# The sample's rows of a differential attention: both components' queries in one stationary operand, one softmax for 128 rows, summed while the weights are turned

## The chip, the cores and the metric

One NeuronCore of a Trainium2 chip runs one launch of a whole encoder layer. The metric is device time in microseconds, the median of several runs. Engines: PE (TensorE, matmuls; PEld is its weight load), DVE (VectorE), ACT (ScalarE), POOL (GpSimd), SP (SyncE, which issues most DMAs).

## The reference

One layer of a hybrid encoder serves two groups: a prompt of 512 rows and a sample of 64 rows, with shared weights. After a projection the rows go through a gated-delta recurrence and, side by side with it, a differential attention; then come an output projection, an attention to a memory, and a feed-forward block. The change is in the differential attention: 4 heads, each with two components of 64 dimensions.

```python
def one(args):
    qi, pi = args
    s = jnp.einsum('bqhcd,bkhcd->bhcqk', qi.astype(jnp.float32), kf) * scale
    visible = k_pos[None, :] < ((pi // CHUNK + 1) * CHUNK)[:, None]
    s = jnp.where(visible, s, -jnp.inf)
    p = jax.nn.softmax(s, axis=-1)
    a = p[:, :, 0] - lam * p[:, :, 1]
    return jnp.einsum('bhqk,bkhe->bqhe', a, vf)
```

Two softmaxes, one per component, are combined as the first minus lambda times the second, and the result weighs the values. The sample's 64 rows attend to 256 cached keys and their own 64, so 320 keys, all visible.

## The kernel before

Everything is held transposed, with features on the 128 partitions and the 576 rows (512 prompt, then 64 sample) along the free axis. Weights come by DMA in blocks, are split into a high and a low part (`wh` by ACT on L161, `wl` by DVE on L162), and `project` multiplies both with the split rows, in two passes over 256 and 320 rows. The PSUM tile of a projection is called `pr`; its matmuls fill PE whenever nothing else does, and they stand on L107, as every matmul does (helper `mm`). Transposes stand on L113 (helper `tr`, by a multiplication with `ident`). PSUM has eight banks: three `pr`, two `ba`, and one each of `g0`, `g1` and `gs`.

A list scheduler sorts the instructions of each engine by dependences and its own cost estimates. So an edit in one place moves instructions of the neighbours, and each engine then runs its list strictly in order.

For each head `h`, `diff_project(h)` projects queries, keys and values. The sample's queries are copied by ACT (L976) out of the projection into `qz`, component 1 into partitions 0 to 63 of plane 0, component 2 into partitions 64 to 127 of plane 1; the other halves were set to zero by POOL. `qz` has one buffer, so the copies for the next head wait until PE has read it. `diff_head(h)` then takes the sample (t = 4) first, and four prompt tiles of 128 queries (t = 0 to 3). For each tile and component the scores go into bank `g1` or `g0` (component index 1 first), DVE takes the row's maximum (L1052) and scales it (L1053), ACT takes the exponential with the row's sum (L1055) into `p1` or `p0`. DVE inverts the sums (L1057), multiplies component 2's by minus lambda (L1058), scales `p1` (L1059) and adds scaled `p0` to it (L1060). PE turns the combined weights into a `ba` bank in blocks of 128 keys, ACT copies them to `aT` (L1067), PE multiplies with the values into `gs`, and ACT takes the squares' sum (L1075) and copies the rows to `an` (L1076). `finish` normalizes the head's rows (L1079, the POOL power on L208, L1081) and turns them; it runs when the next head reaches t = 1.

For t = 4 the stationary operand is a plane of `qz` with 128 columns: the last 128 rows of the sequence axis, of which the last 64 are the sample's. In parallel with the heads runs the sample's recurrent scan (`sample`), which shares the bank `gs` and ends with the DVE product on L808, behind a POOL power. After head 3, the split rows are turned back (L1107, L1108) and the memory's keys and values follow.

Of the kernel before, what the change touches and what calls it, by code (L numbers as in the profile page):

```python
# [10 lines left out]
AF = mybir.ActivationFunctionType  # L11
# [26 lines left out]
def hybrid_layer_kernel(  # L38
# [53 lines left out]
    def small(tag, shape, bufs=None, dt=F32):  # L92
        tag = SHARED.get(tag, tag)
        bufs = 1 if tag in ("vn", "on", "S", "qz") or tag[:-1] in ("At", "Dt", "Y") else 2
        return sp.tile(shape, dt, tag=tag, name=nm(tag), bufs=bufs)
# [840 lines left out]
    ckT, cvv = cv2[:, 0].rearrange("p b (c n) -> p (b c) n", n=PAST), cv2[:, 1]  # L936

    qs = [cp.tile([P, 2, T], F32R, tag=f"qz{i}", name=nm("qs")) for i in range(2)]
    qz = small("qz", [P, 2, P])
    with tc.issue_after(behind_keys[0]), tc.issue_after(behind_keys[1]):  # L940
        G.memset(qz[64:, 0, :], 0.0)
        G.memset(qz[:64, 1, :], 0.0)
        G.memset(vs[64:], 0.0)
    stacked = {}

    def diff_project(h):
        hs = slice(h * P, (h + 1) * P)
        if h < 2:
            qn = [od[:, 2 * h + j, :SEQ].bitcast(F32R) for j in range(2)]
        else:  # L950
            qn = [small(tag, [P, SEQ], dt=F32R) for tag in ("Y0", "Y1")]
        tags = ("kd", "vb", "X", "KQ") if h % 2 else ("At0", "At1", "Dt0", "Dt1")
        ks = [small(tag, [P, SEQ], dt=F32R) for tag in tags]
        stacked[h] = ks[:2], ks[2:]
        for kind, base in (("q", 2056), ("k", 2568), ("v", 3080)):
            def evac(b, a0, n, more):
                ts_ = slice(a0, a0 + n)
                t0 = slice(a0, min(a0 + n, SEQ))
                n0 = t0.stop - a0

                def parts(dst, src):
                    A.copy(dst[0][:, t0], src[:, :n0])
                    V.tensor_tensor(dst[1][:, t0], src[:, :n0], dst[0][:, t0].bitcast(F32), ALU.subtract)

                if kind == "q":
                    d = b
                    if more is not None:
                        d = qn[1][:, ts_].bitcast(F32)
                    with tc.high_priority():
                        if more is not None:  # L970
                            add_to(d, b, more)
                        parts(qn, d)
                    if a0:
                        for c in range(2):
                            R = slice(64 * c, 64 * c + 64)
                            A.copy(qz[R, c, :], d[R, n - P :])  # L976
                            for j in range(2):
                                nc.sync.dma_start(
                                    qs[h % 2][64 * j : 64 * j + 64, c, :SEQ].bitcast(F32), qn[j][R].bitcast(F32)
                                )  # L980
                    return
                d = small("zr", [P, 320])[:, :n] if kind == "v" else kdT[:, h, ts_]
                with tc.high_priority():
                    if more is not None:
                        add_to(d, b, more)
                    else:
                        V.tensor_copy(d, b)
                if kind == "k":
                    parts(stacked[h][0], d)
                    if a0:  # L990
                        first_, second_ = ([x.bitcast(F32) for x in pair_] for pair_ in stacked[h])
                        for j in range(2):
                            for R in (slice(0, 64), slice(64, P)):
                                nc.sync.dma_start(second_[j][R], first_[j][64:])
                        for j in range(2):
                            nc.sync.dma_start(first_[j][64:], first_[j][:64])
                bt = bank()
                for t in range(2):
                    tr(bt[:, t * P : (t + 1) * P], d[:, t * P : (t + 1) * P])
                if a0:  # L1000
                    tr(bt[:DEC, 256:384], d[:, 256:])
                src, t2 = bt[:, :256].rearrange("p (t d) -> p t d", t=2), slice(a0 // P, a0 // P + 2)
                if kind == "v":
                    A.copy(vtm[:, t2, hs], src)
                    if a0:
                        A.copy(vs[:DEC, h, :], bt[:DEC, 256:384])
                else:
                    ko = small("ko", [P, 3, P])
                    A.copy(ko[:, :2], src)
                    nc.sync.dma_start(o_dk_p[0, 0, a0 : a0 + 256, h, :].rearrange("(t p) d -> p t d", p=P), ko[:, :2])  # L1010
                    if a0:
                        A.copy(ko[:DEC, 2], bt[:DEC, 256:384])
                        nc.sync.dma_start(o_dk_s[0, 0, :, h, :], ko[:DEC, 2])

            project(weights(w2, base + h * P), xs, evac)
        nc.sync.dma_start(o_dv_p[0, 0, :, h, :].rearrange("(t p) d -> p t d", p=P), vtm[:, :, hs])
        nc.sync.dma_start(o_dv_s[0, 0, :, h, :], vs[:DEC, h, :])

    def diff_cache():
        ckr = [small("p0", [P, 512]), small("p1", [P, 512])]  # L1020
        nc.sync.dma_start(cvv, cache_diff_v[0, 0].rearrange("(b p) h d -> p b (h d)", p=P))
        for bi in range(2):
# [3 lines left out]
                tr(b[:, h * P : (h + 1) * P], ckr[bi][:, h * P : (h + 1) * P])  # L1026
            A.copy(ckT[:, :, bi * P : (bi + 1) * P], v4(b, 4))

    def diff_head(h, between):


        hs = slice(h * P, (h + 1) * P)
        so, co = tiny([P, 5], "ta"), tiny([P, 5], "ta")
        on = small("an", [P, 5, P])
        for t in (4, 0, 1, 2, 3):
            if t == 1:
                between()
            q0 = QT[t][0]
            nk = q0 + P if t < 4 else PAST + DEC
            nb = (nk + P - 1) // P  # L1040
            pr = {}
            mx, l = tiny([P, 2], "ta"), tiny([P, 2], "ta")
            for c in (1, 0):
                b = bank(f"g{c}")
                if t < 4:
                    for j in range(2):
                        mm(b[:, :nk], qs[h % 2][:, c, q0 : q0 + P], stacked[h][c][j][:, :nk], start=j == 0, stop=j == 1)
                    V.memset(b[:64, nk - 64 : nk], -1e30)
                else:
                    mm(b[:, :PAST], qz[:, c, :], ckT[:, h, :])  # L1050
                    mm(b[:, PAST:nk], qz[:, c, :], kdT[:, h, SEQ:T])
                V.tensor_reduce(mx[:, c : c + 1], b[:, :nk], AX.X, ALU.max)  # L1052
                V.tensor_scalar(mx[:, c : c + 1], mx[:, c : c + 1], -0.125, None, ALU.mult)  # L1053
                p = small(f"p{c}", [P, 512])
                A.activation(p[:, :nk], b[:, :nk], AF.Exp, bias=mx[:, c : c + 1], scale=0.125, accum_out=l[:, c : c + 1])  # L1055
                pr[c] = p
            V.reciprocal(l, l)  # L1057
            V.tensor_tensor(l[:, 1:2], l[:, 1:2], nlam, ALU.mult)  # L1058
            V.tensor_scalar(pr[1][:, :nk], pr[1][:, :nk], l[:, 1:2], None, ALU.mult)  # L1059
            V.scalar_tensor_tensor(pr[0][:, :nk], pr[0][:, :nk], l[:, 0:1], pr[1][:, :nk], ALU.mult, ALU.add)  # L1060
            if nk < nb * P:
                G.memset(pr[0][:, nk : nb * P], 0.0)
            bt = bank()
            aT = small("aT", [P, 4, P])
            for kb in range(nb):
                tr(bt[:, kb * P : (kb + 1) * P], pr[0][:, kb * P : (kb + 1) * P])
            A.copy(aT[:, :nb, :], v4(bt, nb))  # L1067
            po = bank("gs")[:, :P]
            for kb in range(nb):
                if t < 4:  # L1070
                    vv = vtm[:, kb, hs]
                else:
                    vv = cvv[:, kb, hs] if kb < 2 else vs[:, h, :]
                mm(po, aT[:, kb, :], vv, start=kb == 0, stop=kb == nb - 1)
            A.activation(pr[1][:, :P], po, AF.Square, accum_out=so[:, t : t + 1])  # L1075
            A.copy(on[:, t, :], po)  # L1076

        def finish():
            V.tensor_scalar(so, so, 1.0 / P, EPS, ALU.mult, ALU.add)  # L1079
            rpow(co, so)  # L1080
            V.tensor_tensor(on, on, co.unsqueeze(2).to_broadcast([P, 5, P]), ALU.mult)  # L1081
            b, b2 = bank(), bank()
            for t in range(4):
                tr(b[:, t * P : (t + 1) * P], on[:, t, :])
            tr(b2[:, :P], on[:, 4, :])
            for src, ts_ in ((b, slice(0, SEQ)), (b2[:, DEC:P], slice(SEQ, T))):
                A.activation(od[:, h, ts_], src, AF.Identity, scale=dn)

        return finish
# [566 lines left out]
```

## Time and profile before

| | |
|---|---|
| median of 3 runs | 982.89 us (981.1 to 982.91) |
| profiled execution | 983.15 us, span 981.0 us, granted PE clock 0.998 |
| PE busy | 963.2 us (98 %) |
| PEld busy | 889.8 us (91 %) |
| DVE busy | 695.8 us (71 %) |
| ACT busy | 541.2 us (55 %) |
| POOL busy | 57.5 us (6 %) |
| PE on the chain that ended last | 59 % of the span, 38 % of it projection matmuls (`pr`) |
| the four heads of the differential attention | about 250 to 367 us |

Read the shares as averages over stages. In the timeline, a row has a start, a duration, the engine, the line, the operation and `output<-inputs`, with `xN` records; `[x <-engine line]` at its end is idle time ahead of the row and what ended it. A plain f32 matmul leaves two records, a transpose or an `f32r` matmul one.

### The profile page before, as it was taken

The numbers are of one execution on the slowest core, as the hardware profiler recorded it, in microseconds if no ns is written. First come the engines' busy times: TensorE is split into PE (matmuls) and PEld (weight loads), VectorE is DVE, ScalarE is ACT, GpSimd is POOL, SyncE is SP. The second block draws the span as 40 slices with busy tenths as digits, with TensorE's granted clock in tenths as the row PEclk, the third lists the DMA queues.
The fourth block names the chain that finished last, engine by engine and source line by source line (L and its number), as shares of the span: only waits on it lengthen the run. The fifth ranks groups of instructions, "written<-read, shape, count | busy, mean of one in ns | idle before, by whom it ended". The sixth has DMA issues, their size and how long they took to land.

```text
span 981.0 us, 17018 instructions
## 1 busy us (share of the span) xinstructions
PE 963.2 (98%) x6403; PEld 889.8 (91%) x6403; DVE 695.8 (71%) x1552; ACT 541.2 (55%) x1226; POOL 57.5 (6%) x122
## 2 busy tenths in 40 slices
PE   9999999999999999999999999999999999999996
PEld 7999999888888778999999998999999999999996
DVE  6655777867777687666657887567767779978674
ACT  7665785434557675435445567665544455544444
POOL 3441010101000000000000000000000000000000
PEclk9999999999999999999999999999999999999999
DMA  7442432121644756341121523222222222322202
GB/s 212 121 129 76 113 105 65 33 55 45 173 132 126 232 164 193 87 129 44 44 64 44 140 73 89 88 86 87 86 86 86 87 87 87 87 87 86 65 23 96
DMA packets 124915, 96.01 MB, mean 98 GB/s; under 512 B 6204, under 2 KB 112846, under 8 KB 124322
## 3 DMA queue, kind: packets, MB, share of 16 engines
q1 hardware_dynamic: 124466, 94.28, 33.2%
q8 instruction: 50, 0.82, 0.3%
q10 hardware_dynamic: 368, 0.66, 0.2%
q14 instruction: 31, 0.25, 0.1%
HBM read 79.93 MB, written 9.75 MB: 91 GB/s over the span
## 4 chain that ended last, share of the span: by engine, by line
PE 59%; issue 2%; DVE 2%; ACT 1%; DMA 1%; POOL 0%; POOLq 0%; ACTq 0%; DVEq 0%; SPq 0%
PE pr L107 38%; PE ba L107 10%; PE g L107 6%; PE gs L107 4%; PE ba L113 1%; DMA r<-in_w_ff_dram 1%; DMA raw<-in_w_ff_dram 0%; ACT c L1448 0%; ACT u L1539 0%; DVE w L1302 0%; ACT w2h L1402 0%; ACT c L1447 0%; DVE u L1495 0%; ACT keep L1438 0%; DVE w2l L1403 0%
## 5 line engine op out<-in xcount | busy, mean ns | idle before, releaser
L107 PE MATMUL pr<-u,wh 128*128 128x320 f32 (+2 forms) x1240 | 326.0, 341 | 1.3 <-DVE zr L195 0.9
L107 PEld LDWEIGHTS pr<-u,wh 128*128 128x128 f32 x1240 | 211.5, 188 | 16.3 <-DVE zr L195 1.1
L107 PE MATMUL pr<-u,wl 128*128 128x256 f32 (+1 forms) x816 | 225.9, 300 | 0.0
L107 PEld LDWEIGHTS pr<-u,wl 128*128 128x128 f32 x816 | 150.0, 189 | 2.2 <-DVE wl L388 0.2
L162 DVE TENSOR_TENSOR wl<-raw,wh 128x1024 fp32r<-128x1024 f32 x65 | 79.5, 1223 | 51.5 <-ACT wh L161 51.3
L161 ACT CAST wh<-raw 128x1024 fp32r<-128x1024 f32 x65 | 68.3, 1050 | 58.1 <-PE pr L107 41.4
L107 PE MATMUL pr<-u,w2h 128*128 128x320 f32 (+1 forms) x384 | 98.6, 340 | 0.0
L1402 ACT CAST w2h<-r 128x512 fp32r<-128x512 f32 x56 | 34.7, 619 | 89.5 <-PE pr L107 86.3
L107 PE MATMUL pr<-f,w2h 128*128 128x320 f32 (+1 forms) x288 | 74.6, 341 | 0.8 <-DVE u L1489 0.7
L107 PEld LDWEIGHTS pr<-u,w2h 128*128 128x128 f32 x384 | 65.0, 188 | 4.6 <-issue 0.4
L107 PE MATMUL pr<-u,w2l 128*128 128x256 f32 (+1 forms) x256 | 65.2, 295 | 0.0
L1487 DVE TENSOR_TENSOR u<-u,pr 128x256 f32<-128x256 f32 x96 | 42.2, 448 | 17.0 <-PE pr L107 16.4
L107 PE MATMUL ba<-u,wl 128*128 128x288 f32 x360 | 53.0, 296 | 1.0 <-ACT keep L1438 0.9
L107 PEld LDWEIGHTS pr<-f,w2h 128*128 128x128 f32 x288 | 48.7, 188 | 5.2 <-issue 2.0
L107 PEld LDWEIGHTS ba<-u,wl 128*128 128x128 f32 x360 | 49.2, 188 | 1.7 <-ACT keep L1438 1.6
L107 PE MATMUL pr<-f,w2l 128*128 128x256 f32 (+1 forms) x192 | 48.8, 295 | 0.0
L107 PEld LDWEIGHTS pr<-u,w2l 128*128 128x128 f32 x256 | 46.9, 188 | 1.5
L208 POOL TENSOR_TENSOR tiny<-tiny,nhalf 128x1 f32<-128x1 f32 (+4 forms) x10 | 9.3, 932 | 645.2 <-DVE tiny L1555 532.2
L1403 DVE TENSOR_TENSOR w2l<-r,w2h 128x512 fp32r<-128x512 f32 x56 | 38.5, 687 | 11.3 <-ACT w2h L1402 11.0
L107 PE MATMUL pr<-wh,u 128*128 128x512 f32 x128 | 43.3, 403 | 0.0
L1447 ACT ACTIVATE c<-c 128x288 f32<-128x288 f32 x48 | 20.6, 443 | 29.4 <-DVE c L1446 29.4
L107 PEld LDWEIGHTS pr<-f,w2l 128*128 128x128 f32 x192 | 35.2, 188 | 1.1
(536 smaller groups left out, 2032.0 us busy)
## 6 DMA issues: line engine op xcount, KB each, us to landing
raw<-in_w_ff_dram SPq DMA_DIRECT2D x36, 512.0 KB
raw<-in_w_in_dram SPq DMA_DIRECT2D x28, 512.0 KB
r<-in_w_ff_dram SPq DMA_DIRECT2D x56, 256.0 KB
raw<-in_w_mem_k_dram SPq DMA_DIRECT2D x8, 512.0 KB
raw<-in_w_mem_v_dram SPq DMA_DIRECT2D x8, 512.0 KB
raw<-in_w_out_dram SPq DMA_DIRECT2D x8, 512.0 KB
raw<-in_w_mem_q_dram SPq DMA_DIRECT2D x8, 512.0 KB
raw<-in_w_mem_o_dram SPq DMA_DIRECT2D x8, 512.0 KB
```

The source lines that it names most:

```text
L107: i = nc.tensor.matmul(out, lhsT, rhs, start=start, stop=stop, skip_group_check=skip_group_check)
L113: i = nc.tensor.transpose(out, in_, ident[:n, :n])
L161: A.copy(wh, raw)
L162: V.tensor_tensor(wl, raw, wh.bitcast(F32), ALU.subtract)
L208: G.tensor_tensor(out, in_, bc(nhalf[: in_.shape[0], 0:1], list(in_.shape)), ALU.pow)
L1402: A.copy(wh, src)
L1403: V.tensor_tensor(wl, src, wh.bitcast(F32), ALU.subtract)
L1447: A.activation(c, c, AF.Relu)
L1487: V.tensor_tensor(am, am, b, ALU.add)
```

## The change

For the sample's rows, `diff_head` calls a new function. `qz` is now one 128 x 128 operand in two diagonal blocks: component 1's 64 queries in rows and columns 0 to 63, component 2's in 64 to 127. Its product with the keys gives the scores of both components in one bank, component 1 in the upper 64 rows and component 2 in the lower. One maximum, one exponential, one reciprocal and one scaling then serve all 128 rows, the lower 64 with minus lambda. The two components are added by the turn: instead of a transpose (multiplication by the identity), a plain f32 matmul multiplies by `both`, whose columns 64 to 127 hold an identity for the upper rows and one for the lower, and whose other columns are zero. The result has the sample's rows in columns 64 to 127 of `aT`, as before, and zeros in the rest. What follows is unchanged, but for the name of the buffer that takes the squares. Prompt tiles are computed as before.

```diff
-    qz = small("qz", [P, 2, P])
+    qz = small("qz", [P, P])
+    both = const([P, P], "both")
     with tc.issue_after(behind_keys[0]), tc.issue_after(behind_keys[1]):
-        G.memset(qz[64:, 0, :], 0.0)
-        G.memset(qz[:64, 1, :], 0.0)
+        G.memset(qz[64:, :64], 0.0)
+        G.memset(qz[:64, 64:], 0.0)
+        G.memset(both[:, :64], 0.0)
+        for c in range(2):
+            G.tensor_copy(both[64 * c : 64 * c + 64, 64:], ident[64 * c : 64 * c + 64, 64 * c : 64 * c + 64])
...
-                            A.copy(qz[R, c, :], d[R, n - P :])
+                            A.copy(qz[R, R], d[R, n - DEC :])
...
+    def sample_rows(h, hs, so, on):
+
+        nk = PAST + DEC
+        mx, l = tiny([P, 1], "ta"), tiny([P, 1], "ta")
+        b = bank("g1")
+        mm(b[:, :PAST], qz, ckT[:, h, :])
+        mm(b[:, PAST:nk], qz, kdT[:, h, SEQ:T])
+        V.tensor_reduce(mx, b[:, :nk], AX.X, ALU.max)
+        V.tensor_scalar(mx, mx, -0.125, None, ALU.mult)
+        p = small("p1", [P, 512])
+        A.activation(p[:, :nk], b[:, :nk], AF.Exp, bias=mx, scale=0.125, accum_out=l)
+        G.memset(p[:, nk : 3 * P], 0.0)
+        V.reciprocal(l, l)
+        V.tensor_tensor(l[64:], l[64:], nlam[64:], ALU.mult)
+        V.tensor_scalar(p[:, :nk], p[:, :nk], l, None, ALU.mult)
+        bt = bank()
+        aT = small("aT", [P, 4, P])
+        for kb in range(3):
+            mm(bt[:, kb * P : (kb + 1) * P], p[:, kb * P : (kb + 1) * P], both)
+        A.copy(aT[:, :3, :], v4(bt, 3))
+        po = bank("gs")[:, :P]
+        for kb in range(3):
+            mm(po, aT[:, kb, :], cvv[:, kb, hs] if kb < 2 else vs[:, h, :], start=kb == 0, stop=kb == 2)
+        sq = small("p0", [P, 512])
+        A.activation(sq[:, :P], po, AF.Square, accum_out=so[:, 4:5])
+        A.copy(on[:, 4, :], po)
...
+            if t == 4:
+                sample_rows(h, hs, so, on)
+                continue
```

The order of PE's instructions moves with it. In these rows `g_472` is bank `g1`, `g_474` bank `g0`, `u_76` the cached keys and `u_78` the sample's own keys. First the sample's scores in head 0, before:

```order
L107 MATMUL pr_3435<-u_93,wh_3431 128x512
L107 MATMUL g_472_2785<-u_76,qz_2545 128x256
L107 MATMUL g_472_2785<-u_78,qz_2545 128x64
L107 MATMUL g_474_2792<-u_76,qz_2545 128x256
L107 MATMUL g_474_2792<-u_78,qz_2545 128x64
L107 MATMUL pr_3435<-u_93,wl_3432 128x256
```

And the same place in the changed kernel:

```order
L107 MATMUL pr_3425<-u_93,wh_3421 128x512
L107 MATMUL g_472_2789<-u_76,qz_2545 128x256
L107 MATMUL g_472_2789<-u_78,qz_2545 128x64
L107 MATMUL pr_3425<-u_93,wl_3422 128x256
L107 MATMUL pr_3425<-u_93,wh_3421 128x512
```

Two of the four matmuls are gone, and projection matmuls follow at once. Next the turn of the sample's weights in head 0, behind the scores of the first prompt tile (`qs` is the prompt's queries, `At` and `Dt` the stacked keys), before:

```order
L107 MATMUL g_483_2826<-At_433_2549,qs_2543 128x128
L107 MATMUL g_483_2826<-At_434_2550,qs_2543 128x128
L107 MATMUL pr_3435<-u_94,wl_3432 128x256
L107 MATMUL pr_3435<-u_94,wh_3431 128x512
L107 MATMUL pr_3462<-u_93,wh_3431 128x320 x2
L107 MATMUL pr_3462<-u_93,wl_3432 128x320
L107 MATMUL pr_3462<-u_93,wh_3431 128x320 x2
L113 MATMUL ba_2804<-ident,p_475_2797 128x128 x3
L107 MATMUL pr_3462<-u_93,wl_3432 128x320
```

And in the changed kernel:

```order
L107 MATMUL pr_3425<-u_94,wh_3421 128x512
L107 MATMUL g_480_2815<-Dt_435_2555,qs_2543 128x128
L107 MATMUL g_480_2815<-Dt_436_2556,qs_2543 128x128
L107 MATMUL g_482_2823<-At_433_2553,qs_2543 128x128
L107 MATMUL g_482_2823<-At_434_2554,qs_2543 128x128
L107 MATMUL ba_2800<-both,p_473_2794 128x128 x3
L107 MATMUL pr_3452<-u_93,wh_3421 128x320 x2
L107 MATMUL pr_3452<-u_93,wl_3422 128x320
L107 MATMUL pr_3452<-u_93,wh_3421 128x320
L107 MATMUL gs_2806<-u_76,aT_2801 128x128 x2
```

The turn now stands directly behind the scores of the first prompt tile, with no projection matmuls between. Last, PE at the start of head 1, where the last tile of head 0 (`ba` from `p_511`, then `p_510`) and the first of head 1 (`X`, `KQ`, `kd`, `vb` are its stacked keys) meet, before:

```order
L107 MATMUL gs_2906<-u_78,aT_2901 128x128 x3
L107 MATMUL pr_3535<-u_94,wl_3508 128x320
L107 MATMUL pr_3535<-u_94,wh_3507 128x320 x2
L107 MATMUL pr_3535<-u_94,wl_3508 128x320 x2
L113 MATMUL ba_2934<-ident,p_511_2928 128x128 x4
L113 MATMUL ba_3044<-ident,u_78 128x128 x2
L107 MATMUL g_559_3209<-X_2955,qs_2544 128x128
L107 MATMUL g_559_3209<-KQ_2956,qs_2544 128x128
L107 MATMUL gs_2941<-u_78,aT_2935 128x128 x4
L113 MATMUL ba_3084<-ident,u_78 128x128 x2
```

And in the changed kernel:

```order
L107 MATMUL g_559_3207<-kd_2950,qs_2544 128x128
L107 MATMUL g_559_3207<-vb_2951,qs_2544 128x128
L107 MATMUL pr_3525<-u_94,wh_3497 128x320
L107 MATMUL pr_3525<-u_94,wl_3498 128x320
L107 MATMUL pr_3525<-u_94,wh_3497 128x320
L107 MATMUL g_557_3199<-X_2952,qs_2544 128x128
L107 MATMUL g_557_3199<-KQ_2953,qs_2544 128x128
L107 MATMUL pr_3525<-u_94,wh_3497 128x320
L107 MATMUL pr_3525<-u_94,wl_3498 128x320
L113 MATMUL ba_2931<-ident,p_510_2925 128x128 x4
L113 MATMUL ba_3041<-ident,u_78 128x128 x2
L107 MATMUL pr_3525<-u_94,wl_3498 128x320
```

Both components' scores of head 1's first tile now stand ahead of the six transposes, component 1 (`kd`, `vb`) first, and projection matmuls follow these.

More of the change, by code (lines that the diff above doesn't have):

```diff
@@ L1044, in diff_head @@
                 b = bank(f"g{c}")
[L1045 to L1051, printed above, removed]
+                for j in range(2):
+                    mm(b[:, :nk], qs[h % 2][:, c, q0 : q0 + P], stacked[h][c][j][:, :nk], start=j == 0, stop=j == 1)
+                V.memset(b[:64, nk - 64 : nk], -1e30)
                 V.tensor_reduce(mx[:, c : c + 1], b[:, :nk], AX.X, ALU.max)
@@ L1060, in diff_head @@
             V.scalar_tensor_tensor(pr[0][:, :nk], pr[0][:, :nk], l[:, 0:1], pr[1][:, :nk], ALU.mult, ALU.add)
-            if nk < nb * P:
-                G.memset(pr[0][:, nk : nb * P], 0.0)
             bt = bank()
@@ L1069, in diff_head @@
             for kb in range(nb):
[L1070 to L1074, printed above, removed]
+                mm(po, aT[:, kb, :], vtm[:, kb, hs], start=kb == 0, stop=kb == nb - 1)
             A.activation(pr[1][:, :P], po, AF.Square, accum_out=so[:, t : t + 1])
```

## The prediction, made before the run

> **What bounds the kernel now.** I read the page first: the busy shares, then the chain that ended last.
>
> ```profile
> PE 963.2 (98%) x6403; PEld 889.8 (91%) x6403; DVE 695.8 (71%) x1552; ACT 541.2 (55%) x1226; POOL 57.5 (6%) x122
> ...
> PE 59%; issue 2%; DVE 2%; ACT 1%; DMA 1%; POOL 0%; POOLq 0%; ACTq 0%; DVEq 0%; SPq 0%
> ```
>
> TensorE (PE) is busy for 98 % of the span, and no other engine takes more than 2 % of the chain. So PE is the bound: a microsecond less of PE work is worth a microsecond only if PE does not spend it waiting. Next I took the busy time by stage around the differential attention, and there the list of what PE waits for (window 250 to 370 us).
>
> ```profile
> 270.00:290.00 20.00, 18.75 (x123) 16.68 (x122) 14.07 (x46) 11.71 (x39) 1.99 (x3) 1.00 0.59 162
> 350.00:370.00 20.00, 18.90 (x105) 14.98 (x104) 15.96 (x33) 14.69 (x34) 1.17 (x1) 1.00 0.45 140
> ```
>
> ```profile
> PE ba L113 <- DVE At L1108: 1.1, 1, 1.1
> PE gs L107 <- DVE on L808: 1.0, 1, 1.0
> PE gs L107 <- ACT aT L1067: 0.3, 1, 0.3
> ```
>
> In each row of the first fence the second number after the window is PE's busy time out of 20 us, the third PEld's, the fourth DVE's. The only real holes of PE in this region are 1.25 us in one stage and 1.1 us in another, and the second fence names them: three waits, 2.4 us together. The clock column is 1.00 in both rows, so no term below comes from the clock.
>
> **The change part by part.** *Scores.* PE's timeline in head 0, with start, duration and number of records:
>
> ```profile
> 255.88 1.52 PE L107 MATMUL g<-u,qz 128*128 128x256 f32 x8
> 257.21 0.36 PE L107 MATMUL pr<-u,wl 128*128 128x256 f32 x1
> ...
> 259.40 0.34 PE L107 MATMUL g<-Dt,qs 128*128 128x128 f32 x2
> ...
> 261.18 0.55 PE L113 MATMUL ba<-ident,p 128*128 128x128 f32 x3
> 261.48 0.39 PE L107 MATMUL pr<-u,wl 128*128 128x320 f32 x1
> ...
> 262.29 0.71 PE L107 MATMUL gs<-u,aT 128*128 128x128 f32 x4
> 262.84 0.39 PE L107 MATMUL gs<-vs,aT 128*128 128x128 f32 x2
> 262.98 0.39 PE L107 MATMUL pr<-u,wh 128*128 128x320 f32 x1
> ```
>
> Matmuls overlap in their modelled ends, so I take the time from one group's start to the next group's start. A plain f32 matmul shows as two records, a transpose as one. The eight records of the sample's scores, both components, take 257.21 − 255.88 = 1.33 us; half of them, 0.67 us, goes. In head 1 the second component has a run of its own:
>
> ```profile
> 273.82 0.87 PE L107 MATMUL g<-u,qz 128*128 128x256 f32 x4
> ...
> 275.05 0.77 PE L107 MATMUL g<-u,qz 128*128 128x256 f32 x4
> 275.63 0.39 PE L107 MATMUL pr<-u,wh 128*128 128x320 f32 x1
> 275.86 0.86 PE L107 MATMUL gs<-u,aT 128*128 128x128 f32 x6
> 276.48 0.39 PE L107 MATMUL pr<-u,wl 128*128 128x320 f32 x1
> ...
> 277.87 0.32 PE L107 MATMUL g<-X,qs 128*128 128x128 f32 x1
> 278.02 0.28 PE L107 MATMUL g<-KQ,qs 128*128 128x128 f32 x1
> 278.57 1.16 PE L107 MATMUL gs<-u,aT 128*128 128x128 f32 x8 [0.27 <-ACT aT L1067]
> ```
>
> That is 0.58 us. The mean of the two, 0.62 us, for four heads: **−2.5 us** of PE work.
>
> *Turn of the weights.* Three transposes take 261.48 − 261.18 = 0.30 us. Three plain f32 matmuls of the same shape are not shown with `both`, but the run with `aT` is the nearest row: six records in 262.98 − 262.29 = 0.69 us in head 0, 276.48 − 275.86 = 0.62 us in head 1. The least they could cost is what the transposes cost, since they push the same three tiles of 128 columns; that bound gives 0. I take the rows nearest in kind, 0.66 − 0.30 = 0.36 us a head: **+1.4 us**, at most 4 × 0.39 = 1.6.
>
> The Trainium skill, page "Perfetto Trace Analysis", section "Transposes", speaks against this edit: a logical transposition should be issued as a transpose and not as a standard matmul, because transposes skip the arithmetic. The trace agrees, 0.30 against 0.62 to 0.69 us for three tiles; with matmuls as cheap as transposes the sum below would be 1.4 us lower.
>
> PE's own work so falls by 2.5 − 1.4 = **1.1 us**.
>
> *VectorE and ScalarE.* By shape, window 250 to 350 us:
>
> ```profile
> L1055 ACT ACTIVATE p<-g,ta 128x320 f32<-128x320 f32 x8 | 4.3, 534 | 0.7 <-DVE ta L1053 0.5
> ...
> L1052 DVE TENSOR_REDUCE ta<-g 128x1 f32<-128x320 f32 x8 | 3.9, 488 | 0.3
> ...
> L1057 DVE RECIPROCAL ta<-ta 128x2 f32<-128x2 f32 x18 | 2.9, 163 | 6.8 <-ACT p L1055 6.5
> ...
> L1060 DVE SCALAR_TENSOR_TENSOR p<-p,ta,p 128x320 f32<-128x320 f32 x4 | 2.2, 546 | 0.1
> ...
> L1059 DVE TENSOR_SCALAR p<-p,ta 128x320 f32<-128x320 f32 x4 | 1.6, 388 | 0.1
> ```
>
> Each head loses one reduction (0.49 us) and the combining instruction (0.55 us) on DVE and one exponential (0.53 us) on ACT. Neither engine is the bound in the stages above, so this is worth nothing by itself; it shortens the chain from scores to turned weights.
>
> *GpSimd.* Three more instructions stand among the masks near 52 us, and head 0's zeroing of the last 64 columns now stands ahead of a square root instead of behind it.
>
> ```profile
> 56.82 0.11 POOL L314 MEMSET p<- 128x3 f32 x1 [1.03 <-DVE p L457]
> ...
> 128.31 0.56 POOL L208 TENSOR_TENSOR tiny<-tiny,nhalf 128x1 f32<-128x1 f32 x1 [29.82 <-DVE tiny L228]
> ```
>
> Both are covered: GpSimd idles 1.03 us soon after the first place and 29.82 us before the second, and the zeroed buffer's former users are the convolution's, done before that idle time. Without that cover they would cost a few tenths.
>
> *Waits that go.* In head 1 the run at 278.57 follows the record at 278.02, whose neighbour took 0.15 us to the next start; so about 0.4 us of those 0.55 is a wait for the ScalarE copy of `aT`, because the matmuls came four instructions behind the transposes that they need. In the new order four projection matmuls stand between, so it goes: **−0.4 us**. The larger one is this:
>
> ```profile
> 288.26 0.16 DVE L806 TENSOR_TENSOR tg<-tg,tg 128x2 f32<-128x2 f32 x1 [0.81 <-POOL tg L208]
> 288.45 0.86 DVE L808 TENSOR_TENSOR on<-gs,tg 64x256 f32<-64x256 f32 x2
> 289.35 0.42 DVE L195 TENSOR_TENSOR Y<-pr,Y 128x256 f32<-128x256 f32 x1
> ...
> 289.46 0.68 PE L107 MATMUL gs<-u,aT 128*128 128x128 f32 x4 [0.98 <-DVE on L808]
> ```
>
> Here the sample's weighted values need the `gs` bank, of which only one exists, and the recurrent sample scan still reads it (L808), behind a GpSimd square root. The change touches neither. PE now arrives later, since the longer turn (0.36 us) stands ahead and four scores records went; but in the new order DVE has the addition L195 (0.42 us), which stood behind L808, ahead of it. I give this **−0.2 us**, with 0 and −1.0 as the ends. The third wait, for L1108 at the end of head 3, hangs on a GpSimd square root and stays.
>
> *Waits that come.* Everything shorter is also packed closer. In head 0 the turn stands 15 projection matmuls and four scores matmuls behind the sample's scores. Twelve projection matmuls took 259.40 − 257.21 = 2.19 us before, 0.18 each; 15 of them behind a run of 0.67 us from 255.88, and four scores matmuls at 0.15 us (278.02 − 277.87), put PE at the turn at 259.9. The weights are ready when DVE has gone through this, in the new order too with the low half of a weight (L162) between the maximum and its scaling:
>
> ```profile
> 257.19 1.22 DVE L162 TENSOR_TENSOR wl<-raw,wh 128x1024 fp32r<-128x1024 f32 x1
> ...
> 258.33 0.15 DVE L1053 TENSOR_SCALAR ta<-ta 128x1 f32<-128x1 f32 x1
> ```
>
> From 258.5 an exponential (0.53), a reciprocal and a product with lambda (0.16 for the one, taken for the other too) and the scaling (0.39) add up to 1.24 us, so 259.75, or about 260.0 with the handing over between engines. So **0 to 0.3 us** of waiting, where there was none. In head 1 it is the exponential itself that comes late:
>
> ```profile
> 273.65 0.70 ACT L1055 ACTIVATE p<-g,ta 128x512 f32<-128x512 f32 x1
> ...
> 275.25 0.48 ACT L1067 COPY aT<-ba 128x384 f32<-128x384 f32 x1 [0.82 <-PE ba L113]
> 275.86 0.53 ACT L976 COPY qz<-pr 64x128 f32<-64x128 f32 x2
> ...
> 277.17 0.54 ACT L1055 ACTIVATE p<-g,ta 128x320 f32<-128x320 f32 x1
> ```
>
> Before, the last tile's 0.70 us exponential ran at 273.65, ahead of the copy at 275.25. In the new order it stands behind that copy and one `qz` copy, and the sample's exponential behind all of them, so it still ends near 277.5. The next tile's scores for component 2 (`g1`), which in the old order started at 277.87 behind six transposes, now stand ahead of those. From 273.82 on PE has three transposes (0.3), the scores (0.6), the values' run (0.6), seven projection matmuls (7 × 0.18) and the pair for `g0` (0.3) to do, and is there near 276.9. They wait for bank `g1`, hence **0.5 to 0.85 us**. Queued behind it on PE are the transposes of the last tile and the projection. Heads 2 and 3 have the same edits with slacker neighbours. I take **+0.8 us** for all new waits, with 0 and 4.6 (all four heads at 0.85 + 0.3) as the ends.
>
> **Sum:** −1.1 − 0.4 − 0.2 + 0.8 = −0.9 us, against the profiled execution's 983.15: 982.25. The median of the three runs, 982.89, lies 0.26 us below it; the forecast is made against the median, 982.89 − 0.9 = **982.0 us**. A measurement of this kernel can tell about 0.2 % (2.0 us) from no change, so this counts as the same.
>
> **The rivals.** *All holes close.* The new waits are nil, and L808's wait goes whole, because PE comes over a microsecond later or the scan's square root sooner. Then −1.1 − 0.4 − 1.0 = −2.5: 980.4 us. For it speaks that head 0's new wait is near zero by the walk; against it that nothing shortens the chain DVE, GpSimd, DVE ahead of L808.
>
> *One bank takes the place of two.* The sample's scores all go to `g1`; the next tile's scores in `g1` cannot start before the only exponential has read 320 columns. At the upper end, 4 × (0.85 + 0.3) = 4.6, the sum is −1.1 − 0.4 − 0.2 + 4.6 = +2.9: 985.8 us, slower. It decides from new waits of 3.7 us on, since −1.7 + 3.7 = 2.0. Head 1's ScalarE rows speak for it; against it, the new order in heads 1, 2 and 3 puts the tile's other component (`g0`) first, and before the change a wait for an exponential is not in PE's list at all. The Trainium skill, "Perfetto Trace Analysis", section "Matmuls", has the rule behind this: independent matmul groups should rotate through different PSUM banks, so that one is emptied while the next is filled. No run here shows yet what one bank costs.
>
> *It doesn't do what it says.* The removed run was no time on the path, since what PE saves it waits for at L808 and L1108 (2.1 us of waits that end by other engines). Then only the matmuls ahead of neither count, and the sum is about 0 to −0.5: 982.4 to 982.9. It lies inside the forecast's case.
>
> **How the numbers follow.** The forecast's case, new waits between 0 and 3.7 us with the L808 wait mostly kept (981.0 to 984.9, the last rival in it): 0.48. All holes close, or nearly: 0.31. One bank, slower: 0.21. Faster by over 0.2 % therefore 0.31, within 0.48, slower 0.21. The range for 8 in 10 goes from 979.9, the first rival with another half microsecond, to 985.5, just short of the second rival's end.
>
> **What would show it.** Right: in the new trace the sample's scores run takes about 0.65 us, the turn 0.6 to 0.7, with 0.3 us or less ahead of it in head 0; the 278.57 wait is gone; a wait of 0.5 us or more for the sample's exponential stands ahead of `g<-X,qs` in head 1; the L808 wait is still 0.7 us or more; PE's busy time falls by about 1 us. Wrong: a wait of over 0.5 us ahead of the turn in each head, a turn that takes over 0.8 us, or a difference that lies outside 250 to 375 us, where no term of mine has its place.

## The result, and the profile after

The changed kernel takes 979.32 us (median of six runs, 978.39 to 979.89). The kernel before took 982.58 us beside it (six runs, 980.86 to 983.24). The ratio is 0.9972, with a 95 % interval of 0.9962 to 0.9982: faster by 1.8 to 3.7 us. I had forecast 982.0, that is no difference that can be told, with a range down to 979.9. The measured time lies 0.6 us below that. The sign of the sum was right; it came out about 2 us too small.

From the page of the profile after, the span and the line of busy time:

```profile
span 978.2 us, 16971 instructions
...
PE 960.9 (98%) x6399; PEld 889.0 (91%) x6399; DVE 691.4 (71%) x1540; ACT 537.4 (55%) x1218; POOL 57.5 (6%) x125
```

PE is still busy for 98 % of the span and so still the bound. What PE waits for in the changed kernel, window 250 to 370 us:

```profile
PE ba L113 <- DVE At L1132: 1.1, 1, 1.1
PE gs L107 <- DVE on L808: 0.7, 1, 0.7
PE g L107 <- ACT p L1043: 0.4, 1, 0.4
```

The wait for L808 fell from 1.0 to 0.7 us, the one for the copy `aT` (0.3) is gone, the one ahead of the last turn stays (its line is now L1132), and the forecast one for the sample's exponential (L1043) is there. So two of the three old waits are left, and one new one has joined them. PE's timeline in head 0 after the change:

```profile
255.65 0.87 PE L107 MATMUL g<-u,qz 128*128 128x256 f32 x4
256.32 0.36 PE L107 MATMUL pr<-u,wl 128*128 128x256 f32 x1
...
259.22 0.39 PE L107 MATMUL g<-At,qs 128*128 128x128 f32 x2
259.76 0.94 PE L107 MATMUL ba<-both,p 128*128 128x128 f32 x6
260.45 0.54 PE L107 MATMUL pr<-u,wh 128*128 128x320 f32 x2
```

The scores of the sample take 256.32 − 255.65 = 0.67 us where both components took 1.33; the turn takes 260.45 − 259.76 = 0.69 us where the transposes took 0.30. And in head 1, where the new waits were expected:

```profile
275.72 0.31 PE L107 MATMUL pr<-u,wh 128*128 128x320 f32 x1
276.39 0.33 PE L107 MATMUL g<-X,qs 128*128 128x128 f32 x1 [0.36 <-ACT p L1043]
...
289.42 0.68 PE L107 MATMUL gs<-u,aT 128*128 128x128 f32 x4 [0.69 <-DVE on L808]
```

To compare kernels I measure a **stage**: from the first record of the sample's scores in head 0 to one projection row shortly behind the attention. These are the end rows, of before, of the changed kernel, and, with its first row, of a second profile of before (the first experiment below):

```profile
390.01 0.28 PE L107 MATMUL pr<-u,wl 128*128 128x256 f32 x1
```

```profile
387.82 0.28 PE L107 MATMUL pr<-u,wl 128*128 128x256 f32 x1
```

```profile
256.36 1.52 PE L107 MATMUL g<-u,qz 128*128 128x256 f32 x8
...
390.44 0.28 PE L107 MATMUL pr<-u,wl 128*128 128x256 f32 x1
```

Before: 390.01 − 255.88 = 134.13 us. Changed: 387.82 − 255.65 = 132.17 us, **1.96 us less**. Second profile of before: 390.44 − 256.36 = 134.08 us. So in this one pair of profiles the stage repeats to 0.05 us, far finer than the total time does, and the experiments are read from it. Ahead of the stage and behind it PE's records stand in the same order in all the programs below.

"PE work" in the table is the start-to-start time of the sample's scores and turns over all four heads in a program's own trace, less that of before. In the changed kernel the scores take 2.40 us where they took 4.98, that is −2.58. The turns take 0.69, 0.59, 0.59 and 0.59 us where they took 0.30, 0.25, 0.28 and 0.27, that is +1.36; so −1.22 us in all. (The expectations below reckon with 1.5 for the turn and −1.05 in all.) "Rest" is what is left: waits, and short gaps between unlike matmuls. The medians come from several series, in which before took between 981.90 and 982.58 us, so the text gives ratios.

| kernel | stage, us | against before | PE work | rest | median, us |
|---|---|---|---|---|---|
| before | 134.13 | | | | 982.58 |
| before again | 134.08 | −0.05 | −0.02 | −0.03 | 981.48 |
| changed | 132.17 | −1.96 | −1.22 | −0.74 | 979.32 |
| changed, scores twice | 134.42 | +0.29 | +1.33 | −1.04 | 981.54 |
| changed, transposes kept | 132.51 | −1.62 | −2.49 | +0.87 | 978.76 |
| changed, load given back | 132.61 | −1.52 | −1.12 | −0.40 | 980.43 |
| transposes, changed order | 131.55 | −2.58 | −2.64 | +0.06 | 977.92 |
| changed in the old order | 134.10 | −0.03 | −1.24 | +1.21 | 982.17 |
| sum at the eviction | 131.01 | −3.12 | −2.51 | −0.61 | 977.49 |
| the same, changed order | 132.91 | −1.22 | −2.64 | +1.42 | 979.22 |
| turn by matmul, old order | 135.37 | +1.24 | +1.49 | −0.25 | 982.62 |
| before, components swapped | 133.95 | −0.18 | +0.07 | −0.25 | 981.8 |
| changed, components swapped | 133.09 | −1.04 | −1.11 | +0.07 | 980.73 |
| sum at eviction, swapped | 131.37 | −2.76 | −2.54 | −0.22 | 977.9 |

### The profile page after: what moved, and what is told of

Read it like the earlier page. It is cut to its first block, busy times and chain, and to the rows that moved or that the text cites. A ratio compares the mean times of both kernels' runs of the same rounds, so it can differ in the third digit from the quotient of the medians.

```text
span 978.2 us, 16971 instructions
## 1 busy us (share of the span) xinstructions
PE 960.9 (98%) x6399; PEld 889.0 (91%) x6399; DVE 691.4 (71%) x1540; ACT 537.4 (55%) x1218; POOL 57.5 (6%) x125
## 4 chain that ended last, share of the span: by engine, by line
PE 86%; DVE 5%; ACT 3%; issue 2%; DMA 2%; POOL 1%; POOLq 0%; ACTq 0%; DVEq 0%; SPq 0%
PE pr L107 53%; PE g L107 11%; PE ba L107 10%; PE gs L107 6%; PE ba L113 3%; PE g L113 2%; DMA raw<-in_w_ff_dram 1%; DMA r<-in_w_ff_dram 1%; POOL tg L208 1%; DVE wl L162 1%; DMA raw<-in_w_mem_o_dram 1%; ACT wh L161 0%; DVE w L1326 0%; PE gs L113 0%; DVE on L808 0%
## 5 line engine op out<-in xcount | busy, mean ns | idle before, releaser
L162 DVE TENSOR_TENSOR wl<-raw,wh 128x1024 fp32r<-128x1024 f32 x65 | 79.5, 1223 | 56.0 <-ACT wh L161 55.8
```

The lines of the kernel that those rows point to most:

```text
L162: V.tensor_tensor(wl, raw, wh.bitcast(F32), ALU.subtract)
```

## The experiments

Three theories stand in the expectations. Theory 1: the gain is PE's own work. Theory 2: the gain comes from the shorter chain on VectorE and ScalarE. Theory 3: the order that the scheduler finds decides, and what PE saves it may spend waiting.

**Before again.** No edit.

> The kernel before, run as if it were a new one: a second profile of the same program. Every theory expects no difference (ratio 1.000 within 0.1 %). What it tells is how far two profiles of one program differ from 393 us on, where nothing was changed: there the pair of before and after differed by 0.65 us. If two profiles of the same program differ there by 0.5 us or more, that part of the gain is no effect of the change; if by 0.1 us, it has to be explained.

Measured: 981.48 us, ratio 0.9999 (0.999 to 1.0008). The span of the first profile of before is 981.0 us and that of the second this one:

```profile
core 0 of [0], span 978.9 us
```

From the stage's end row to the end of the span the first takes 981.0 − 390.01 = 590.99 us, the second 978.9 − 390.44 = 588.46, and the changed kernel 978.2 − 387.82 = 590.38. What PE waits for from 540 to 980 us, first in the first profile of before, then in the second:

```profile
PE ba L107 <- ACT keep L1438: 1.2, 2, 0.9
PE pr L107 <- DVE u L1489: 0.7, 2, 0.5
```

```profile
PE ba L107 <- ACT keep L1438: 0.2, 1, 0.2
```

The same program got 2.5 us shorter behind the attention from one profile to the next, 1.7 of it in these waits, and stayed the same in the stage. So these profiles cannot show the 0.6 us by which before and after differ there as an effect of the change. One small place looks alike in most changed programs: a gap of 0.23 us ahead of the transposes at 478.52 us of before is shorter by 0.17 us in the changed kernel, but also by 0.18 us in a version of before with the same work (components swapped, below).

**Scores twice.**

```diff
         mm(b[:, PAST:nk], qz, kdT[:, h, SEQ:T])
+        again = bank("g0")
+        mm(again[:, :PAST], qz, ckT[:, h, :])
+        mm(again[:, PAST:nk], qz, kdT[:, h, SEQ:T])
```

> The changed kernel with a second run of the sample's scores per head into bank g0, read by nobody: PE gets back the work that the change removed, VectorE and ScalarE do not. Theory 1 (the gain is PE's own work): PE gains 2.6 us of work, so about 982.0 us, 0.6 us below the kernel before. Theory 2 (the gain is the shorter chain on VectorE and ScalarE, PE's records only fill gaps): at most 1 us slower than the changed kernel, 980.3 us or less.

Measured: 981.54 us, ratio 0.9995 (0.9987 to 1.0004); the stage is 2.25 us longer than in the changed kernel, for about 2.55 us of added work. Theory 1's figure was 982.0. The order moved too: the 1.1 us wait ahead of the last turn is not in this program's list, and one of 0.6 us for the low half of a weight (L162) is new. So this fits theory 1, but it is not the price of the scores alone.

**Transposes kept**, the sum left out.

```diff
-            mm(bt[:, kb * P : (kb + 1) * P], p[:, kb * P : (kb + 1) * P], both)
+            tr(bt[:, kb * P : (kb + 1) * P], p[:, kb * P : (kb + 1) * P])
```

> The changed kernel with three transposes of the weights in place of the three matmuls with the doubled identity; the sum of the two components is left out, so the rows of the sample are not the reference's. Theory 1: PE has 1.5 us less to do, so 977.8 us, 4.8 us below before. Theory 2 or a theory that waits take what PE saves: as the changed kernel, 979.3 us.

Measured: 978.76 us (ratio 0.997, 0.9959 to 0.998), and a stage 0.34 us longer than the changed kernel's, though PE has 1.27 us less to do. The scheduler chose another order from the sample's values in head 1 on, and in it a new wait stands in head 2, where the first component's scores come straight behind the second's:

```profile
316.11 0.40 PE L107 MATMUL g<-Dt,qs 128*128 128x256 f32 x2
317.04 0.50 PE L107 MATMUL g<-At,qs 128*128 128x256 f32 x2 [0.53 <-ACT p L1085]
```

So the saved work went into waits elsewhere. That spoke for theory 3, and later runs tie the order.

**Load given back.**

```diff
+        idle, idle2 = tiny([P, 1], "ta"), tiny([P, 1], "ta")
+        V.tensor_reduce(idle, b[:, :nk], AX.X, ALU.max)
+        spare = small("p0", [P, 512])
+        A.activation(spare[:, :nk], b[:, :nk], AF.Exp, bias=mx, scale=0.125, accum_out=idle2)
...
+        V.scalar_tensor_tensor(spare[:, :nk], spare[:, :nk], l, p[:, :nk], ALU.mult, ALU.add)
```

> The changed kernel with a second reduction, a second exponential and a second scaling-and-adding of 128x320 per head, into a buffer read by nobody: VectorE and ScalarE get back the work that the change took from them, PE's work stays as changed. Theory 1: as the changed kernel, 979.3 us within 0.5. Theory 2: the waits that closed open again, 1 to 2.5 us slower than the changed kernel, 980.3 to 981.8 us.

Measured: 980.43 us, ratio 0.9985 (0.9976 to 0.9994); the stage is 0.44 us longer than in the changed kernel. The time lies in theory 2's range, but the stage shows less than theory 2's 1 us, and the rest lies where the total wanders. So the relief of VectorE and ScalarE may not be worth nothing, as I had it, but under half a microsecond of the stage here; the edit moves the order too, so even that is not its price alone.

**Transposes in the changed kernel's order.** As "transposes kept", with all PE instructions of the stage chained in the order of the changed kernel, by edges that hold the order of issue only:

```diff
+        wanted = [traced[k] for a, n in parts for k in range(a, a + n)]
+        for i, ahead in zip(wanted[1:], wanted):
+            tc.add_manual_dep(i, ahead.name, ...)
```

> As the run with the transposes kept (the sum of the components left out), but PE's instructions are tied to the order that the changed kernel has, so that only the kind of twelve of them differs. Theory 1 (PE's work decides): the stage from 254 to 393 us of the kernel before gets 1.5 us shorter than in the changed kernel, that is 3.4 us shorter than before. Theory 3 (what PE saves it waits for in this order too): between 0 and 0.5 us shorter than in the changed kernel.

Measured: 977.92 us, ratio 0.9958 (0.9945 to 0.997), a stage 0.62 us shorter than the changed kernel's, for 1.42 us less work. It lies between the theories, nearer to theory 3. PE's waits show where the rest went:

```profile
PE gs L107 <- DVE on L808: 1.1, 1, 1.1
PE ba L113 <- DVE At L1132: 1.1, 1, 1.1
PE g L107 <- ACT p L1043: 0.4, 1, 0.4
PE gs L107 <- ACT aT L1052: 0.3, 1, 0.3
```

PE reaches the `gs` bank in head 1 sooner and waits 0.4 us longer for L808, and 0.3 us for a copy that the longer turn had covered.

**The changed computation in the old order.** The same chain, with PE's order taken from before.

> The changed kernel's computation with PE's instructions tied to the order of the kernel before (the second component's scores taken out of it, the turn's matmuls where the transposes stood). Theory 1 with the new order as the source of the closed waits: the stage from 254 to 393 us is 1.05 us shorter than before (PE's work alone), 0.9 us longer than in the changed kernel. Theory 2 (the shorter chain on VectorE and ScalarE closes the waits): 1.9 us shorter than before in the old order too.

Measured: 982.17 us, ratio 1.0004 (0.9995 to 1.0013), a stage of 134.10 us: nothing of the change is left. Both theories said more, 1.05 and 1.9 us. PE's waits in it:

```profile
PE gs L107 <- ACT aT L1095: 1.1, 4, 0.4
PE ba L113 <- DVE At L1132: 1.1, 1, 1.1
PE gs L107 <- DVE on L808: 0.6, 1, 0.6
PE g L107 <- DMA X<-in_cache_mem_v_dram: 0.5, 1, 0.5
PE g L107 <- ACT p L1043: 0.3, 1, 0.3
PE ba L113 <- DVE p L1090: 0.2, 1, 0.2
```

Against before, three named waits come new, 1.0 us together, and the one for the copy `aT` grows from 0.3 to 1.1 us in four places; L808's falls by 0.4. With PE's work shorter and its order unchanged, PE runs into what VectorE, ScalarE and the stacking of the keys deliver. The row behind L808 shows it:

```profile
289.96 0.68 PE L107 MATMUL gs<-u,aT 128*128 128x128 f32 x4 [0.63 <-DVE on L808]
```

From the stage's start this row begins after 33.54 us here (289.96 − 256.42), after 33.58 us in before and after 33.77 us in the changed kernel. So in the old order, less PE work ahead of the row does not move it. In the changed kernel the row is no earlier either, but 61 projection matmuls of 128x320 stand ahead of it where the old order has 54. The new order puts seven more of them, about 1 us, into the time that was saved; in the old order PE waits. So the work alone gives nothing of the 1.96 us; what the new order would give with the old work, no run tells.

**Sum at the eviction.** The whole computation, with transposes:

```diff
-            mm(bt[:, kb * P : (kb + 1) * P], p[:, kb * P : (kb + 1) * P], both)
-        A.copy(aT[:, :3, :], v4(bt, 3))
+            tr(bt[:, kb * P : (kb + 1) * P], p[:, kb * P : (kb + 1) * P])
+        A.copy(aT[:, :3, :64], v4(bt, 3)[:, :, :64])
+        V.tensor_tensor(aT[:, :3, 64:], v4(bt, 3)[:, :, 64:], aT[:, :3, :64], ALU.add)
```

> The changed kernel with transposes for the turn, and the two components added when the turned weights leave PSUM: ScalarE copies component 1's columns, VectorE adds component 2's to them (the whole computation is done). The scheduler chooses the order. Theory 1: 1.5 us less PE work than the changed kernel, so 977.8 us. Theory 3: the order that the scheduler finds decides, as in the run with the transposes: within 0.6 us of the changed kernel's 979.3.

Measured: 977.49 us (977.18 to 978.32), ratio 0.9955 (0.9943 to 0.9967), the fastest of all. Theory 1 said 977.8. PE's, ScalarE's and VectorE's rows at the turn in head 0:

```profile
259.89 0.55 PE L113 MATMUL ba<-ident,p 128*128 128x128 f32 x3
...
260.19 0.54 PE L107 MATMUL pr<-u,wh 128*128 128x320 f32 x2
...
260.47 0.32 ACT L1052 COPY aT<-ba 128x192 f32<-128x192 f32 x1 [0.80 <-PE ba L113]
...
260.82 0.36 DVE L1053 TENSOR_TENSOR aT<-ba,aT 128x192 f32<-128x192 f32 x1 [0.47 <-ACT aT L1052]
```

The turn takes 0.30 us of PE, and the sum costs one VectorE instruction of 0.36 us, while ScalarE's copy is half as wide.

**The same in the changed kernel's order.**

> As the run before this one, with PE's instructions tied to the changed kernel's order. Theory 1: 977.8 us, or 0.3 us more for the second instruction in the eviction ahead of the values' matmuls in each head. Theory 3: 979 to 980 us, since PE then waits for the longer eviction in four places.

Measured: 979.22 us, ratio 0.9973 (0.9962 to 0.9983); the stage is 1.90 us longer than in the scheduler's own order, and 0.74 us longer than the changed kernel's. PE's waits:

```profile
PE gs L107 <- DVE on L808: 1.6, 1, 1.6
PE ba L113 <- DVE At L1133: 1.1, 1, 1.1
PE gs L107 <- DVE aT L1053: 1.0, 3, 0.6
PE g L107 <- ACT p L1043: 0.4, 1, 0.4
```

The values' matmuls wait for the two-step eviction in three places, and in head 1 for L808, 1.6 us. As theory 3 had it, but for a program that is slower only in this order.

**Turn by matmul, old order.** Before, with `mm(..., ident)` in place of `tr` for t = 4, in before's order.

> The kernel before with the sample's three transposes per head replaced by plain f32 matmuls with the identity, PE's order tied to that of before: 1.5 us more PE work and nothing else. Theory 1 (work counts one for one): the stage from 254 to 393 us is 1.5 us longer. Theory 3 (in a given order, work fills or opens waits): less than 1 us longer, since three of the four turns stand ahead of waits that end by VectorE.

Measured: 982.62 us, ratio 1.0001 (0.9992 to 1.0011), which by itself tells nothing; the stage is 1.24 us longer for 1.49 us of work. Theory 3's "less than 1 us" is missed, theory 1's 1.5 nearly met. The wait for L808 shrank to 0.6 us in it.

**Components swapped**, in before, in the changed kernel, and in the sum at the eviction: `for c in (0, 1)` in place of `for c in (1, 0)` in the prompt tiles (in before, whose loop is shared, for the sample's rows too), the scheduler choosing the order.

> The kernel before with the components taken in the other order (0, then 1): the same work on every engine, another order of some 400 PE instructions. Theory 1: the stage from 254 to 393 us as before, within 0.3 us. Theory 3: it moves by 0.5 to 1.5 us, either way, as much as the change itself.

> The changed kernel with the prompt tiles' components taken in the other order: the same work as the changed kernel, another order. Theory 1: the stage as in the changed kernel (1.95 us shorter than before) within 0.3 us. Theory 3: 0.5 to 1.5 us from it, either way.

> The version with transposes and the sum at the eviction, with the components of the prompt tiles in the other order. Theory 1: as the version itself (977.5 us), within 0.3 us. Theory 3: 977 to 979 us.

Measured: 981.8, 980.73 and 977.9 us, ratios 0.9994 (0.9984 to 1.0003), 0.9985 (0.9976 to 0.9994) and 0.9956 (0.9939 to 0.9972). For the same work the stage moves by 0.18 us for before, 0.92 us for the changed kernel and 0.36 us for the third. So theory 1's 0.3 us holds for the first and theory 3 for the second; the third, at 977.9, misses theory 1's 977.5 by 0.4 us and lies in theory 3's 977 to 979. In the swapped order the changed kernel's gain in the stage is 1.04 us against before, about its PE work of 1.11, and 0.86 us against before swapped.

Taken together: the rest column runs from −1.04 to +1.42 us over these orders, and its mean over all twelve edited programs (second profile of before left out) is +0.01 us. The stage follows PE's work, give or take what the order makes of the waits; the two largest values belong to orders taken over from another program.

## Why the prediction was right or wrong

*PE's work* was right: −1.1 us forecast, −1.22 measured, with the scores at −2.58 (−2.5 forecast) and the turn at +1.36 (+1.4). The Trainium skill's rule on transposes ("Perfetto Trace Analysis", "Transposes") is borne out: matmuls in their place cost 1.24 us of the stage in the old order and 0.62 us in the changed kernel's, and the fastest version gives the transposes back.

*Waits that come* were about right. In head 0 the turn's weight load stands idle for 0.29 us until VectorE has scaled the weights (L1047):

```profile
259.76 0.74 PEld L107 LDWEIGHTS ba<-both,p 128*128 128x128 f32 x6 [0.29 <-DVE p L1047]
```

In head 1 `g<-X,qs` is late by 0.5 us from start to start (0.36 in the waits). Together that is 0.8, where +0.8 was taken. The forecast places were hit. Two smaller ones had not been walked: 0.28 us at 293.81 in head 1, and 0.24 us at 327.75 in head 3, which is again `g<-X,qs` close behind the end of the sample's exponential:

```profile
293.30 0.40 PE L107 MATMUL pr<-u,wh 128*128 128x512 f32 x1
293.81 0.30 PE L113 MATMUL ba<-ident,p 128*128 128x128 f32 x1
```

```profile
327.06 0.54 ACT L1043 ACTIVATE p<-g,ta 128x320 f32<-128x320 f32 x1
```

```profile
327.75 0.33 PE L107 MATMUL g<-X,qs 128*128 128x128 f32 x1
```

In the first of these fences a projection row that takes 0.24 us from start to start elsewhere takes 0.51.

*Waits that go* is the step that failed. I named two, −0.4 and −0.2 us, and both came as forecast (the copy's gone, L808's down 0.3). But the rest of −0.74 us is what is left after 0.8 us of new waits (1.3 with the two small ones), so 1.5 to 2.0 us of old ones went, not 0.6. I had read the list of waits, which leaves out what is short; others were in before's timeline, at 310.21, 332.00, 339.61 and 347.38 us, about 0.2 us each:

```profile
309.76 0.39 PE L107 MATMUL pr<-u,wh 128*128 128x512 f32 x1
310.21 0.44 PE L107 MATMUL g<-At,qs 128*128 128x128 f32 x2
```

This row takes 0.45 us to the next start where such a row takes 0.24 elsewhere: 0.21 us of waiting that no line of the list shows. Counted from PE's starts, what is left of it lies in many gaps below 0.15 us where matmuls of different kinds meet; among projection matmuls, plain f32 matmuls and transposes the kind changes 159 times in the stage before and 150 times after. Which of these gaps went because of which edit is not settled.

*VectorE and ScalarE* were priced at nothing; given back, their work cost 0.44 us of the stage, in an order that had changed as well, so the price alone stays open.

*The range* was too tight at its low end for a second reason: it came from the stage alone. The stage accounts for 1.96 us, the short gap at 478 us for 0.17 more; the ratio says 1.8 to 3.7, with its middle at 2.75. Of the remaining 0.6 us no profile shows a cause, and two profiles of the same program differ by more than that behind the attention.

*The rivals.* "All holes close" had nearly the time (980.4) but not the mechanism: L808's wait stayed. "One bank takes the place of two" is refuted as a price: the wait for the sample's exponential is there in head 1, at 0.5 us from start to start, and in head 3, at 0.24, not in four heads at 0.85. The Trainium skill's rule on rotating PSUM banks ("Perfetto Trace Analysis", "Matmuls") agrees with these two waits. Putting `g0` first did not remove them, since in both heads it is first. "It doesn't do what it says" is what happens in the old order: there PE waits for all that it saves.

## What to carry to other kernels

Where the bound engine's work is cut by a microsecond in a list that a scheduler sorts, price the work from the trace, and give the order of the rest a range of its own, here about a microsecond either way; a list of named waits does not hold it. Judge such a change by a stage of the trace between two fixed rows, which repeated to 0.05 us here, not by a total that wanders by 2 us. And a matmul that does a transpose's work for the sake of a sum can give the sum to the instruction that empties the bank. That was worth another 1.16 us of the stage in the order that the scheduler found for it, and cost 0.74 us in the changed kernel's order; the ratios of the whole, 0.9955 and 0.9972, have intervals that overlap.

## What was not expected of the hardware

Two profiles of one program agreed to 0.05 us in the stage and kept their distance to 0.03 us between 100 and 254 us. Yet they drifted up to 0.7 us apart within the first 13 us, and behind the stage one took 2.5 us less than the other, 1.7 of it where PE waits for ScalarE's `keep` and VectorE's `u`. The granted clock was 0.998 in both, so the clock does not explain it. The second profile was taken on chip 1, and on which chip the first was taken is not known; what the cause is, no run here tells.
